# Feature-major gated attention, two heads to a product, and products of ones ahead of the first data

## The chip, the core and the metric

The kernel runs on one core of one Trainium2 chip. The metric is the time of one execution on the device in microseconds (us), from its first to its last instruction and the little that lies around them; the profile's span is that stretch without what lies around it. Everything is float32 at the interface.

## What is computed

A decoder trunk of two layers on 512 tokens with 1,024 features. Layer 0 is the one that the change touches most. Its mixer projects the normed tokens with one matrix, and the columns go to two mixers: gated linear attention (GLA: 4 heads, 64 key and 128 value features, chunks of 64 tokens) and differential attention (4 heads, two softmax maps each). Layer 1 is a dilated sliding-window attention. After each mixer comes a gated MLP with a causal convolution of width 3. The GLA, cut from the reference:

```
qc, kc, vc, lc = chunk(q * (dk ** -0.5)), chunk(k), chunk(v), chunk(log_a)   # chunks of 64 tokens
b = jnp.cumsum(lc, axis=3);  b_last = b[:, :, :, -1:, :]
q_d = qc * jnp.exp(b);  k_d = kc * jnp.exp(-b)
att = jnp.where(causal, einsum('bhnik,bhnjk->bhnij', q_d, k_d), 0.0)
kv = einsum('bhnjk,bhnjv->bhnkv', kc * jnp.exp(b_last - b), vc)
state = exp(b_last) * state + kv                                             # scan over chunks
o = att @ vc + q_d @ state
log_a = log_sigmoid(ar @ w_a2 + b_a) / 16                                    # ar: 16 low-rank features
oa = rmsnorm(o, gla_gain) * silu(ag)
```

The root mean square of a token scales its row of every projection; it is applied after the product.

## The kernel before, in words

**Precision and products.** Each large product is made from three float32r products: every operand is split into a rounded part and the rest (`hi`, `lo`), and hi x hi, lo x hi and hi x lo are added up in one PSUM bank. `split` (line 198) does it with one ScalarE copy and one vector subtraction; `load_next` (166) does the same for each slab of weights, 128 x 1024 in most cases, that a transfer on SP's queue brings. Three raw, three hi and three lo slabs are held, and `slab` (186) keeps two loads ahead. The small products of the attentions are plain float32; each of them is two instructions in the trace, a transpose is one.

**Order.** TensorE's instructions run in the order in which the program issues them; the other engines' order is laid out by the framework. The program interleaves the attentions with the projections by a queue of events: `at(delay, fn, tag)` (279) puts a function into a heap at a time `now + delay`, `pe(us)` (287) lets `now` go on by the planned cost of products, `run` (290) issues a projection step by step and, after each step, fires what is due, and `drain` (295) fires the rest of one kind. `now` is a count of planned TensorE work, and no clock.

**Token-major projections** (`tok_gemm`, 303): tokens are the stationary side, 512 weight columns move, four banks hold the four tiles of 128 tokens; in each of the four slabs the tiles are the outer loop, the slab's two chunks of features the inner one. A step is one tile of one slab, six products. **Feature-major projections** (`feat_gemm`, 325): weights are the stationary side, the 512 tokens move; 24 products for 8 chunks go to one bank. Its step is one bank.

**Start** (435 to 456). On SP's queue come the small parameters, the first 128 x 512 chunk of x, the first slab in two halves, the other seven chunks of x and two slabs between them. Each chunk of x is split with its gain into `hhi`, `hlo` before the projections want it; sums of squares are collected in `sqacc` (223), and a product with a column of ones (`Rstd`, 232) gives the reciprocal root by token. For the MLPs `rstd_rows` (248) gives the same as a row on all partitions: a float32 product of a 128 x 128 matrix of ones with `sqacc`, then six passes of 512 columns on the vector engine and ScalarE.

**Mixer of layer 0** (694 to 710). Projections in the order: differential values, queries, keys, GLA keys and queries (`aqk`), half the gates with the 16 low-rank features, GLA values, the other half of the gates; then the output projection in two halves of eight banks with 12 products each, for the differential and for the GLA heads. The softmax events (`diff_scores`, `diff_tr`, `diff_pv`, 486 to 535) run among them, and behind the last of them the GLA events start, once for each tile n of 128 tokens (two chunks):

- `decay1`, `decay2`, `decay3` (555 to 586) run earlier: they transpose the low-rank features, multiply them with `w_a2`, take the log-sigmoid and split it into `la`. `decay3` multiplies each head's log decay, laid out twice (`y2`), with two columns of constants; ScalarE's exponent of it is `dd`, the decay of a whole tile and of its first chunk.
- `gla_sums(n)` (590): eight products of 256 columns with constant triangles as the stationary side (`tri`) and `la` moving give the decay sums, tokens on partitions. Two exponents (`ee`, `eb`), then six vector products with `aqk`: keys and queries, each laid out twice for the two chunks (`ks`, `qs`), and keys for the state (`kd`). Five planned us later follows `gla_tr`, six later `gla_sums(n + 1)`.
- `gla_tr(n)` (621): eight transposes, one copy each by ScalarE and the vector engine; three planned us later
- `gla_att(n)` (628): four products of 128 x 128, one masked copy (`copy_predicated`) into zeros that GpSimd has written; three planned us later, or once values and gates are there,
- `gla_out(n)` (655): four products with the values, for n > 0 four more with the scaled state `Ss`, a copy to `o`; for n < 3 four products `kd` x values and the state's update (four vector instructions), then the scaled state (four); last `head_norm` (467) with its transposes 7.5 planned us later.

The tiles of these events come from one ring of nine buffers of 512 columns (`t2`, 404); in the GLA part eight of them are taken per n.

## Time and profile before

| | |
|---|---|
| median of 3 runs | 1244.42 us (1244.16 to 1244.56) |
| the profiled execution's own time | 1244.83 us |
| its span | 1242.7 us, 15158 instructions |
| TensorE busy | 1230.5 us (99%) |
| vector engine busy | 765.5 us (62%) |
| ScalarE busy | 542.7 us (44%) |
| DMA | 114.56 MB, 92 GB/s on the mean |

The shares are means over stages with different limits. Products are pipelined, so the busy time of one that stands in the trace is longer than the distance from its start to the next one's; distances between starts are what adds up on TensorE. Engine names in the rows: PE is TensorE, PEld its weight loads, DVE the vector engine, ACT ScalarE, POOL GpSimd, SP the queue that issues transfers. `bank` is a PSUM bank.

### The profile page before, as it was taken

What the parts mean: (1) busy time and instruction counts of PE and PEld (TensorE: products, weight loads), DVE (VectorE), ACT (ScalarE), POOL (GpSimd) and SP (SyncE); (2) the same over time, 40 slices, a digit from 0 to 9 for tenths busy, and PEclk for the clock granted to TensorE, in tenths of its full rate; (3) what the DMA queues carried; (4) which work ended last, traced back from release to release, by engine and by line L of the source; (5) the groups of instructions that cost most, each with busy time, mean ns of one, the idle gap of its engine ahead of it and who ended that gap; (6) DMA issues with size and microseconds to landing.
All of it is one profiled execution on the core that took longest, in us unless ns stands there. A gap on an engine that the chain in (4) does not pass through costs nothing.

```text
span 1242.7 us, 15158 instructions
## 1 busy us (share of the span) xinstructions
PE 1230.5 (99%) x5870; PEld 1021.5 (82%) x5870; DVE 765.5 (62%) x1405; ACT 542.7 (44%) x891; POOL 16.5 (1%) x35
## 2 busy tenths in 40 slices
PE   8999999999999999999999999999999999999998
PEld 6887788888888888888888888889888888888887
DVE  6457768777753776366845565543787536773673
ACT  5446554454432443234634554444544324442341
POOL 0000000000000000000000000300000000000000
PEclk9999999999999999999999999999999999999999
DMA  7222121223323332332422223421223323333322
GB/s 249 89 87 68 35 65 38 85 85 102 103 88 99 102 99 88 102 98 64 136 85 87 85 68 102 106 83 51 93 94 102 102 88 99 102 93 94 102 76 93
DMA packets 34487, 114.56 MB, mean 92 GB/s; under 512 B 4423, under 2 KB 5096, under 8 KB 34416
## 3 DMA queue, kind: packets, MB, share of 16 engines
q1 hardware_dynamic: 32256, 110.38, 28.0%
q10 hardware_dynamic: 1296, 2.10, 0.5%
q0 software_dynamic: 864, 1.12, 0.4%
q8 instruction: 46, 0.75, 0.3%
q14 instruction: 25, 0.20, 0.0%
HBM read 110.41 MB, written 2.12 MB: 91 GB/s over the span
## 4 chain that ended last, share of the span: by engine, by line
PE 96%; DVE 2%; DMA 1%; ACT 1%; issue 0%; POOL 0%; SPq 0%; DVEq 0%; ACTq 0%; POOLq 0%
PE bank L720 39%; PE bank L316 26%; PE bank L762 19%; PE bank L332 5%; PE bank L362 2%; PE bank L943 1%; PE bank L493 1%; PE bank L527 1%; PE bank L928 1%; PE bank L866 1%; PE bank L855 0%; PE bank L515 0%; DMA xT<-in_xT_dram 0%; DVE lo L180 0%; ACT p L499 0%; PE bank L584 0%
## 5 line engine op out<-in xcount | busy, mean ns | idle before, releaser
L177 ACT ACTIVATE hi<-raw 128x1024 fp32r<-128x1024 f32 (+2 forms) x209 | 217.1, 1040 | 324.1 <-PE bank L762 143.2
L180 DVE TENSOR_TENSOR lo<-raw,hi 128x1024 fp32r<-128x1024 f32 (+2 forms) x209 | 250.6, 1199 | 155.9 <-ACT hi L177 148.5
L720 PE MATMUL bank<-hhi,hi 128*128 128x512 f32 x704 | 274.7, 390 | 0.0
L720 PE MATMUL bank<-hlo,hi 128*128 128x512 f32 x704 | 273.9, 389 | 0.0
L720 PE MATMUL bank<-hhi,lo 128*128 128x512 f32 x704 | 273.9, 389 | 0.0
L316 PE MATMUL bank<-hi,hhi 128*128 128x512 f32 (+2 forms) x512 | 201.6, 394 | 5.7 <-ACT hi L177 5.5
L316 PE MATMUL bank<-lo,hhi 128*128 128x512 f32 (+2 forms) x512 | 194.7, 380 | 0.0
L316 PE MATMUL bank<-hi,hlo 128*128 128x512 f32 (+2 forms) x512 | 194.4, 380 | 0.0
L720 PEld LDWEIGHTS bank<-hhi,lo 128*128 128x128 f32 x704 | 132.1, 188 | 28.1 <-issue 0.5
L720 PEld LDWEIGHTS bank<-hhi,hi 128*128 128x128 f32 x704 | 132.1, 188 | 27.8 <-issue 0.5
L720 PEld LDWEIGHTS bank<-hlo,hi 128*128 128x128 f32 x704 | 132.1, 188 | 27.4
L762 PE MATMUL bank<-ghi,lo 128*128 128x512 f32 (+1 forms) x358 | 138.0, 385 | 0.0
L762 PE MATMUL bank<-glo,hi 128*128 128x512 f32 (+1 forms) x358 | 138.0, 385 | 0.0
L762 PE MATMUL bank<-ghi,hi 128*128 128x512 f32 (+1 forms) x358 | 138.0, 385 | 0.0
L316 PEld LDWEIGHTS bank<-hi,hhi 128*128 128x128 f32 x512 | 97.3, 190 | 23.1 <-ACT hi L177 5.5
L316 PEld LDWEIGHTS bank<-lo,hhi 128*128 128x128 f32 x512 | 97.0, 190 | 18.7 <-DVE lo L180 0.2
L316 PEld LDWEIGHTS bank<-hi,hlo 128*128 128x128 f32 x512 | 97.4, 190 | 16.2 <-DVE hlo L205 0.5
L767 DVE TENSOR_TENSOR xT<-xT,bank 128x512 f32<-128x512 f32 (+1 forms) x49 | 33.1, 676 | 106.4 <-PE bank L762 106.1
L762 PEld LDWEIGHTS bank<-ghi,lo 128*128 128x128 f32 x358 | 67.2, 188 | 13.6
L762 PEld LDWEIGHTS bank<-ghi,hi 128*128 128x128 f32 x358 | 67.2, 188 | 13.5
L762 PEld LDWEIGHTS bank<-glo,hi 128*128 128x128 f32 x358 | 67.2, 188 | 13.4
L201 ACT ACTIVATE ghi<-cv 128x512 fp32r<-128x512 f32 x44 | 27.8, 631 | 109.4 <-DVE cv L745 109.4
(192 smaller groups left out, 1288.4 us busy)
## 6 DMA issues: line engine op xcount, KB each, us to landing
raw<-in_weights_dram SPq DMA_DIRECT2D x189, 512.0 KB, 3.5
raw<-in_weights_dram SPq DMA_DIRECT2D x16, 384.0 KB, 3.1
xT<-in_xT_dram SPq DMA_DIRECT2D x8, 256.0 KB, 5.3
out_dram<-xT ACTq DMA_DIRECT2D x7, 256.0 KB, 2.0
raw<-in_weights_dram SPq DMA_DIRECT2D x2, 544.0 KB, 3.6
vt<-vs POOLq DMA_DIRECT2D x16, 64.0 KB, 4.1
raw<-in_weights_dram SPq DMA_DIRECT2D x2, 256.0 KB, 3.5
tr<-in_consts_dram SPq DMA_DIRECT2D x1, 256.0 KB, 4.4
```

The lines of the kernel that those rows point to most:

```text
L177: r = A.activation(hi[:, c0:c1], raw[:, c0:c1], AF.Copy)
L180: V.tensor_tensor(out=lo[:, c0:c1], in0=raw[:, c0:c1], in1=hi.bitcast(F32)[:, c0:c1], op=ALU.subtract)
L201: A.activation(hi, src, AF.Copy)
L316: T.matmul(ps[t][:, :n], lhs(a[:, kc], t), b[:, k, :n], start=(kc == 0 and j == 0), stop=(kc == DC - 1 and j == 2))
L332: T.matmul(ps, w[:, k, d * P:(d + 1) * P], r(k), start=(k == 0 and j == 0), stop=(k == nk - 1 and j == 2))
L362: T.transpose(pt[:, h * P:(h + 1) * P], src[:, h * P:(h + 1) * P], ident)
L493: T.matmul(sc[:, :nk], qT[rs, h, n * P:(n + 1) * P], kT[rs, h, :nk], start=True, stop=True)
L527: T.matmul(po[n][:, h * P:(h + 1) * P], wT[:, j * P:(j + 1) * P], bv[:, j, h * P:(h + 1) * P], start=(h == 0 and j == 0), stop=(h == 3 and ...
L720: T.matmul(ps, w[:, kc], r[:, kc], start=(kc == 0 and m == 0), stop=(kc == DC - 1 and m == 2))
L762: T.matmul(ps[:, ts], a[:, k], b[f0 + k][:, ts], start=(k == 0 and m == 0), stop=(k == n - 1 and m == 2))
L767: V.tensor_tensor(out=xT[:, c, ts], in0=xT[:, c, ts], in1=ps[:, ts], op=ALU.add)
L866: T.matmul(sc[:, hs], q[:, h, ts], k[:, h, ts], start=(h == 0), stop=(h == 3))
```

## The change

Its parts, in the order of the diff:

1. The constants' four triangles are laid out anew as four blocks of 128 columns that all move; the columns that `decay3` and the doubled keys and queries needed are gone.
2. The weight slabs of `aqk` are cut by 128 columns and all 1,024 features, for a feature-major projection.
3. A memset fills the last chunk of `hhi` with ones, and nine products of 512 columns with it go into a bank that nobody reads, ahead of all others.
4. `rstd_rows` splits `sqacc` into float32r parts and makes two float32r products with a float32r matrix of ones, in place of one float32 product.
5. The first projection goes chunk by chunk in its first slab (all four tiles of chunk 0, then of chunk 1; the product with the low part of the weights is second); its step there is two products' worth of tiles. `feat_gemm` with eight chunks has four steps to a bank.
6. The first chunk of x comes and is split in two halves, the first slab's load between them.
7. `rows_begin` is an event of layer 0 (nine planned us after the fourth slab of the first projection, the product five later), which makes the row of reciprocal roots; the feature-major `aqk` is scaled with it by the vector engine when a bank is read.
8. `decay3` and `gla_tr` are gone. In `gla_sums` `la` is the stationary side and 512 columns of constants move, twice for each pair of heads f. One exponent, then short vector products for each f: keys for the two chunks, keys for the state (n < 3), queries for each chunk and head of the pair, with the other head's half of the partitions left zero (`qd`), queries for the state (n > 0); the tile's decay is a column of the exponent. Two transposes stay for the state's keys (n < 3). Scores are four products, two of them with 64 stationary columns. Four masked copies take the place of one. State products are of two heads at once, 256 columns, and only the halves that belong together are read; the scaled state is gone. A tile takes six buffers of the ring.

```diff
@@ constants @@
-C_E0, C_E1, C_B, C_SU, C_W0, ... = (C_KEEP + i * P for i in range(11))
+C_TR, _, _, _, C_W0, ... = (C_KEEP + i * P for i in range(11))
...
+    c[:, C_TR:C_TR + 4 * P] = np.concatenate([e0[:, :64], e1, su, b[:, 64:], b[:, :64], cu[:, 64:]], axis=1)
@@ weight_slabs @@
-        tok("ev_w_in", c0, n)
+        if c0 == 0:
+            slabs.extend(("ev_w_in", 0, 0, DC, c * P, P) for c in range(4))
+        else:
+            tok("ev_w_in", c0, n)
@@ trunk_kernel @@
+    V.memset(hhi[:, DC - 1].bitcast(F32), 1.0)
+    warm = bank()
+    for _ in range(9):
+        T.matmul(warm, hhi[:, DC - 1, :P], hhi[:, DC - 1], start=True, stop=True)
+    onesr = per.tile([P, P], F32R, name="onesr")
+    V.memset(onesr.bitcast(F32), 1.0)
-    def rstd_rows():
+    def rstd_rows(hi, lo, parted=False):
         pb = bank()
-        T.matmul(pb, ones.to_broadcast([P, P]), sqacc[0], start=True, stop=True)
+        if not parted:
+            split(hi, lo, sqacc[0], None)
+        for i, v in enumerate((hi, lo)):
+            T.matmul(pb, onesr, v, start=(i == 0), stop=(i == 1))
@@ tok_gemm @@
+            by_chunk = chunkwise and s == 0
+            for step in range(kper * NT // 2):
+                for u in range(2):
+                    k, t = divmod(2 * step + u, NT) if by_chunk else ((2 * step + u) % kper, (2 * step + u) // kper)
...
+                    for j, (a, b) in enumerate(((hhi, whi), (hhi, wlo), (hlo, whi)) if by_chunk else
+                                               ((hhi, whi), (hlo, whi), (hhi, wlo))):
@@ the start @@
-                nc.sync.dma_start(xT[:, c], x[c])
...
+                for t in ((slice(0, 2 * P), slice(2 * P, S)) if c == 0 else (slice(0, S),)):
+                    nc.sync.dma_start(xT[:, c, t], x[c, :, t])
+                    if i == 0:
+                        split(hhi[:, c, t], hlo[:, c, t], xT[:, c, t], gmix[0][:, c:c + 1])
+                    if c == 0 and t.start == 0:
                         load_next()
...
+        def rows_begin():
+            hi, lo = (t2([P, 512], f"sq{x}").bitcast(F32R) for x in ("hi", "lo"))
+            split(hi, lo, sqacc[0], None)
+            at(5.0, lambda: rows.append(rstd_rows(hi, lo, True)), "params")
@@ decay2, decay3 @@
-            y2 = t2([P, 4, 2, 64], "y2")
-            for u in range(2):
-                V.scalar_tensor_tensor(out=y2[:, :, u], in0=heads(y), scalar=0.0, in1=heads(e), ...)
-            split(heads(la[:, t, 0]), heads(la[:, t, 1]), y2[:, :, 0], None)
-            at(4.0, lambda: decay3(t, y2), "gla")
...
+            V.scalar_tensor_tensor(out=y, in0=y, scalar=0.0, in1=e, op0=ALU.min, op1=ALU.subtract)
+            split(la[:, t, 0], la[:, t, 1], y, None)
@@ gla_sums, gla_att @@
+            ks = [t2([P, 512], f"ks{f}") for f in range(2)]
+            for f in range(2):
+                px = bank()
+                for m in range(2):
+                    T.matmul(px, la[:, n, m, f * P:(f + 1) * P], tri, start=(m == 0), stop=(m == 1))
+                ee = t2([P, 512], f"ee{f}")
+                A.activation(ee, px, AF.Exp)
+                q, k = aqk[:, f, ts], aqk[:, 2 + f, ts]
+                V.tensor_tensor(out=ks[f][:, :64], in0=ee[:, :64], in1=k[:, :64], op=ALU.mult)
+                V.tensor_tensor(out=ks[f][:, 64:192], in0=ee[:, 64:192], in1=k, op=ALU.mult)
+                if n < NT - 1:
+                    V.tensor_tensor(out=ks[f][:, 192:320], in0=ee[:, 192:320], in1=k, op=ALU.mult)
+                for c in range(2):
+                    e0 = 320 + 64 * (1 - c)
+                    for e in range(2):
+                        rs = slice(64 * e, 64 * e + 64)
+                        V.tensor_tensor(out=qd[rs, f, c, e], in0=ee[rs, e0:e0 + 64], in1=q[rs, c * 64:c * 64 + 64], ...)
+                if n > 0:
+                    V.tensor_tensor(out=ks[f][:, 320:448], in0=ee[:, 384:512], in1=q, op=ALU.mult)
+                V.tensor_copy(dd[:, n, f:f + 1], ee[:, 511:512])
...
+            at(5.0, lambda: gla_att(n, ks), "gla")
...
+            for f, c in ((0, 1), (0, 0), (1, 0), (1, 1)):
+                T.matmul(pav[:64 * (c + 1), f, c], ks[f][:, 64 * c:64 + 128 * c], qd[:, f, c].rearrange(...), ...)
@@ gla_out @@
+            if n > 0:
+                for f in range(2):
+                    T.matmul(po[:, f * 256:f * 256 + 256], ks[f][:, 320:448], St[:, f].rearrange("p e v -> p (e v)"), ...)
...
+                for f in range(2):
+                    T.matmul(pv[:, f * 256:f * 256 + 256], kd[:, f], av[:, n, f * 256:f * 256 + 256], ...)
```

## Rows read from the trace of the kernel before

**Rows 1.** The page: busy time, share of the span and instructions of TensorE (part 1), and the shares of the chain that ended last, by engine (part 4).
```profile
PE 1230.5 (99%) x5870; PEld 1021.5 (82%) x5870; DVE 765.5 (62%) x1405; ACT 542.7 (44%) x891; POOL 16.5 (1%) x35
...
PE 96%; DVE 2%; DMA 1%; ACT 1%; issue 0%; POOL 0%; SPq 0%; DVEq 0%; ACTq 0%; POOLq 0%
```

**Rows 2.** Busy time by stretch. Columns: stretch (us), its length, then busy us and number of instructions of TensorE (PE), its weight loads (PEld), the vector engine (DVE), ScalarE (ACT) and GpSimd (POOL); granted TensorE clock, share of the DMA engines' time, GB/s.
```profile
0.00:5.47 5.47, 0.00 (x0) 0.00 (x0) 1.65 (x9) 2.63 (x3) 0.89 (x5) 1.00 0.59 180
5.47:13.87 8.40, 8.13 (x17) 5.54 (x18) 6.63 (x9) 7.86 (x12) 0.00 (x0) 1.00 1.04 382
...
107.40:176.05 68.65, 66.77 (x408) 52.29 (x407) 51.05 (x152) 41.15 (x109) 0.00 (x0) 1.00 0.16 47
176.05:231.60 55.55, 54.61 (x378) 49.75 (x377) 46.54 (x109) 24.94 (x43) 2.10 (x4) 1.00 0.18 58
```

**Rows 3.** The list of waits of TensorE from 0 to 255 us. Columns: who waits at which line <- for whom: us in total, times, longest.
```profile
PE bank L515 <- DVE p L505: 1.4, 1, 1.4
PE bank L631 <- DVE xT L338: 0.8, 1, 0.8
PE bank L493 <- ACT dd L586: 0.3, 1, 0.3
...
PE bank L659 <- DVE rs_u L214: 0.2, 1, 0.2
```

**Rows 4.** Instructions in order of time at the start. Columns: start us, us, engine, line, operation, out<-in, count, idle time before it.
```profile
4.79 0.63 ACT L177 ACTIVATE hi<-raw 128x512 fp32r<-128x512 f32 x1 [0.27 <-DMA raw<-in_weights_dram]
...
12.61 0.63 PE L316 MATMUL bank<-lo,hhi 128*128 128x512 f32 x1
...
13.03 0.63 PE L316 MATMUL bank<-hi,hhi 128*128 128x512 f32 x1
...
14.34 0.39 PE L316 MATMUL bank<-hi,hlo 128*128 128x512 f32 x1
...
14.57 0.40 PE L316 MATMUL bank<-lo,hhi 128*128 128x512 f32 x1
```

**Rows 5.** The chain of waits in order of time, one piece of the first MLP: start us, us, what.
```profile
265.28 87.09 PE bank L720 x384
```

**Rows 6.** Instructions in order of time while the low-rank decay is computed (columns as in rows 4).
```profile
126.53 0.95 PE L584 MATMUL bank<-cst,y 128*128 128x2 f32 x8
127.41 0.92 PE L493 MATMUL bank<-kT,qT 64*128 64x384 f32 x4
...
139.53 0.18 ACT L586 ACTIVATE dd<-bank 128x8 f32<-128x8 f32 x1 [2.11 <-PE bank L584]
```

**Rows 7.** Instructions in order of time in the GLA part (columns as in rows 4): the transposes of tile 0, the sums of tile 1, the state product of tile 1.
```profile
182.77 0.60 PE L362 MATMUL bank<-cst,ks 128*128 128x128 f32 x4
...
183.64 0.60 PE L362 MATMUL bank<-cst,qn 128*128 128x128 f32 x4
...
184.00 1.20 PE L595 MATMUL bank<-la,tri 128*128 128x256 f32 x8
...
185.03 0.28 PE L316 MATMUL bank<-hi,hhi 128*128 128x256 f32 x1
...
205.32 1.06 PE L670 MATMUL bank<-av,kd 128*128 128x128 f32 x8
...
206.21 1.06 PE L631 MATMUL bank<-qsT,ksT 128*128 128x128 f32 x8
```

**Rows 8.** Two score products of the differential attention with a contraction of 64 rows, and what follows on TensorE (columns as in rows 4).
```profile
132.97 0.92 PE L493 MATMUL bank<-kT,qT 64*128 64x384 f32 x4
133.81 0.38 PE L527 MATMUL bank<-bv,wT 128*128 128x128 f32 x1
```

**Rows 9.** The vector engine's groups from 176.05 to 217.85 us, shapes apart. Columns: line, engine, operation, out<-in, shapes, count | busy us, mean ns of one | idle time before them.
```profile
L610 DVE SCALAR_TENSOR_TENSOR qs<-eb,cst,aqk 128x256 f32<-128x256 f32 x8 | 3.7, 480 | 0.0
L635 DVE COPY_PREDICATED att<-cst,bank 128x512 f32<-128x512 int32 x4 | 2.9, 733 | 1.1 <-PE bank L631 1.1
L625 DVE COPY qsT<-bank 128x512 f32<-128x512 f32 x4 | 2.8, 688 | 0.1
...
L680 DVE TENSOR_SCALAR Ss<-St,scl 128x128 f32<-128x128 f32 x12 | 2.6, 282 | 0.0
L616 DVE TENSOR_TENSOR kd<-eb,aqk 128x256 f32<-128x256 f32 x6 | 2.3, 420 | 0.0
L677 DVE SCALAR_TENSOR_TENSOR St<-St,dd,bank 128x128 f32<-128x128 f32 x8 | 2.2, 343 | 0.1
```

**Rows 10.** Busy time by stretch within the GLA part (columns as in rows 2).
```profile
176.05:182.77 6.72, 6.72 (x59) 6.72 (x57) 4.69 (x14) 2.44 (x5) 0.00 (x0) 1.00 0.22 78
...
203.53:210.75 7.22, 7.22 (x55) 6.66 (x53) 7.16 (x20) 1.83 (x5) 1.05 (x2) 1.00 0.22 75
...
222.50:231.50 9.00, 9.00 (x45) 7.51 (x44) 6.26 (x12) 2.74 (x5) 0.00 (x0) 1.00 0.29 96
```

**Rows 11.** ScalarE's SiLU of the gates and the table load behind it (columns as in rows 4).
```profile
193.54 1.92 ACT L686 ACTIVATE ag<-ag 128x2048 f32<-128x2048 f32 x1
...
195.47 1.28 ACT L687 ACT_TABLE_LOAD   x1
```

**Rows 12.** TensorE at the row of reciprocal roots of the first MLP (columns as in rows 4).
```profile
264.26 1.02 PE L251 MATMUL bank<-sqacc,cst 128*128 128x512 f32 x2
...
265.36 0.40 PE L720 MATMUL bank<-hhi,lo 128*128 128x512 f32 x1
```

More of the change, by code (lines that the diff above doesn't have):

```diff
@@ L612, in gla_sums, with gla_att @@
+            pe(0.91)
+            at(5.0, lambda: gla_att(n, ks), "gla")
+            if n < NT - 1:
+                at(GTICK, lambda: gla_sums(n + 1), "gla")
+        def gla_att(n, ks):
             kd = None
             if n < NT - 1:
[L614 to L619 removed]
@@ L692, in late, with ev_qk @@
             at(8.0, lambda: scaled(bv, r0)(t, ps), "params")
-        run(tok_gemm(512, nat, late, before))
+        run(tok_gemm(512, nat, late, before, chunkwise=True))
         run(tok_gemm(512, nat, qk_evict(qT, g_dqk, 8, r0, "diff")))
         run(tok_gemm(512, nat, qk_evict(kT, None, 8, r0, "diff", after_k)))
-        run(tok_gemm(512, nat, scaled(aqk, r0)))
+        for d in range(4):
+            def ev_qk(_, ps, d=d):
+                if d < 2:
+                    V.scalar_tensor_tensor(out=aqk[:, d], in0=ps, scalar=0.125, in1=rows[0], op0=ALU.mult, op1=ALU.mult)
+                else:
+                    V.tensor_tensor(out=aqk[:, d], in0=ps, in1=rows[0], op=ALU.mult)
+            run(feat_gemm(DC, P, lambda k: hhi[:, k], lambda k: hlo[:, k], ev_qk))
         run(tok_gemm(272, nat, agr_evict))
@@ L791, in ffn @@
             p0 = up(0), up(NF)
-            bc = rstd_rows()
+            bc = rstd_rows(*(fp.tile([P, S], F32R, name=f"sq{x}", bufs=1) for x in ("hi", "lo")))
             p1 = up(1), up(NF + 1)
```

150 lines of the change are left out of this document (58 added, 92 removed).

## The prediction

> **What bounds the kernel now.** I read the page first: TensorE is busy for 1230.5 of 1242.7 us, and the chain that ended last is TensorE for 96% of it [rows 1]. So only three things move the end: work that leaves TensorE, idle time in front of it, and its clock. The profiled execution took 1244.83 us, 2.1 around its span, and the median of the runs is 1244.42, 0.4 below; I take my sum off the median. About 0.2% (2.5 us) is the least that a measurement of this kernel tells from no change.
>
> Then the stretches that the diff touches [rows 2]. In the first, the 17 products up to 13.87 us take 8.40 us. In the last two the vector engine is busy for 51.05 of 68.65 and 46.54 of 55.55 us. The list of waits gives TensorE 1.4, 0.8, 0.3 and 0.2 us of idle time behind other engines up to 255 us, besides the first product's own [rows 3]. It is small, but it lies just in the stretches from which work is taken.
>
> **The start: products of ones, halved x, order by chunk.** Before 13.87 us two products of 512 columns start 0.42 us apart, after it 0.23 [rows 4]; in a long stretch 384 of them take 87.09 us, 0.227 each [rows 5]. That is 512 columns at 1.2 and at 2.4 GHz, though the granted-clock column of [rows 2] says 1.00 throughout. 17 products at 0.227 would be 3.9 us, so 4.5 us is the most that the clock and the gaps among them can give.
> The first product waits until 5.47 us, for the cast of the first half slab that begins at 4.79 [rows 4]. The memset and the nine products of ones (9 x 0.43 = 3.8 us) can run from about 1.5 to 5.3, before any data is there. The real ones then begin at about 5.4, as before; the halved x brings them perhaps 0.3 forward, and I don't count it. It costs SP's queue one issue more and puts the second half of that chunk behind both halves of the first slab; the second half's products are third in line, so they aren't late. The memsets of the two state tiles (1,536 columns, an estimated 1.6 us) fit into the first 5.47 us, of which the vector engine is busy for 1.65 [rows 2]. If the level rises as long after the first product as it did before (8.4 us), it does so at 9.9. By then 10 real products are through, and the other 86 take 19.5: 29.4 in place of 13.87 + 79 x 0.227 = 31.8. That is **-2.4**. Bounds: the ones count for nothing and only the order helps, -0.3; the level rises before the first real product, and then the transfers decide (their engines' share is 1.04 there [rows 2]) and some 3.5 are gained. I take the value from the one delay that rows show.
>
> **The decay sums by themselves go** (`decay3`, four groups of eight instructions). One group holds TensorE from 126.53 to 127.41, 0.88 us [rows 6]; the others have the same form: 4 x 0.86 = -3.4. ScalarE's exponent behind it (L586) kept that engine idle for 2.11 us before it could run [rows 6], with the next softmax's exponent queued behind it; this is the 0.3 that L493 waits for `dd` and, I think, half of the 1.4 that L515 waits for [rows 3]. -1.0 for those, bounds 0 (less cover in front of the same transposes gives it back) and -1.7. **Together -4.4.** The second copy of the gates (four vector products) goes too, and costs nothing either way.
>
> **Feature-major keys and queries.** 96 products of 512 columns become 96 of 512. Four evictions leave ScalarE and four come to the vector engine, at some 0.7 us, one every 5.4 us of products: each has its own bank, so nobody waits. New is the row of reciprocal roots: a split, two float32r products, and six passes of 512 columns, due some 40 us before the first eviction wants it. What shows is the two products, 0.46, and the break in the stream: **+0.6**. If that cover were gone the passes would be 4 us once.
>
> **Chunk by chunk (the GLA part), on TensorE.** Before, each tile has eight transposes: two groups of four from 182.77 to 183.64, so 0.87 a tile, 3.5 in all [rows 7]; two of them stay in three tiles, 0.65: -2.8. The sums: 184.00 to 185.03 for eight products of 256 [rows 7] against four of 512, 0.91: -0.4 over four tiles. Scores stay at four products of 128 columns, and the state and output products at the same columns, fewer and longer (205.32 to 206.21 for eight): -0.3. TensorE is 54.6 without its 0.94 of waits; so it would need 54.6 - 3.5 = 51.1 us for what takes 55.55 now.
> Two score products a tile have a stationary of 64 columns, which no row of before has. The nearest are those of 64 rows: 0.84 us for two products (132.97 to 133.81 [rows 8]), where their 4 x 384 columns are 0.64 at 2.4 GHz. So a change of shape costs 0 to 0.2 here; I take 0.1 a tile, +0.4, and 51.5 us. The Trainium skill (TensorEngine Tiling (Array Packing), "Key Properties") says that a change of tiling mode drains the engine. By that, two changes a tile at the 0.2 of [rows 8] would make it +1.6 and the sum 1.2 worse; the row agrees that there is such a price.
>
> **The same on the vector engine.** Here 54 instructions become 96, mostly shorter. By means in [rows 9], before: twelve scaled products at 0.48 and ten plain ones at 0.42, four copies at 0.69, four masked ones at 0.73, the state one copy at 0.69 and 8 x 0.34, the scaled state 12 x 0.28, three tiny copies: 23 us. After: from 0.42 at 256 and 0.28 at 128 columns 64 columns are an estimated 0.21. 68 small products and copies then make 15.4, sixteen masked copies an estimated 0.31 (0.73 less 384 columns) 5.0, the state 3.8: 24.2. Neighbours overlap by up to 0.09 (twelve of 0.282 are busy for 2.6 [rows 9]), so the busy time becomes 44 (all of them overlap) to 48 (those that go from one half of the partitions to the other don't), from 46.5. I take 46.
> The idle time of 9.0 us there can't all be used: 2.0 lies in the first stretch, before the first sums are through, 2.7 in the last, when GLA is done [rows 10], and some 2 while ScalarE does the SiLU with its two table loads (the SiLU 1.92, a load 1.28 [rows 11]): 6.5 to 7. 46 + 6.5 = 52.5 against 51.5: a new wait of 1.0. In the middle the engine is already full: 7.16 of 7.22 us [rows 10].
> A second new wait lies in the ring of nine buffers. A tile now takes six of them, in the order keys, keys, exponents, exponents, keys transposed, scores. By the event queue's own costs the sums of tile 2 are issued ahead of the output of tile 1, and the second exponent of tile 2 gets the buffer that this output still reads; so with tile 3 and the output of tile 2. The scores come 1.1 us behind that output and need the exponent (0.6) and half the products (1.1): about 1.0 late, twice: 2.0. **Waits of 3.0 in place of 0.94**, bounds 0 and 7.5 (48 + 9.0 - 51.5 + 2). Part sum: 51.5 + 3.0 - 55.55 = **-1.0**.
>
> **The two rows in the MLPs.** L251 holds TensorE from 264.26 until the second product behind it starts at 265.36 [rows 12]: 1.10 less one product of 0.23 is 0.87; two float32r products are 0.45. Twice: **-0.8**. The split before them is hidden by the 24 products of the second up-projection chunk, 5.4 us; without that cover it costs 1.3 a time.
>
> Sum: -2.4 - 4.4 + 0.6 - 1.0 - 0.8 = -8.0; 1244.4 - 8.0 = **1236.4**.
>
> **Rivals.**
> *The vector engine becomes the bound of the GLA part, and the kernel gets slower.* Place: the 96 short instructions between the first sums and the last output. If the fixed part of a short instruction is larger than from [rows 9], every 0.1 on it is 9.6 us on an engine that is already full there. It decides from 8.0 + 2.5 = 10.5 us on, 0.32 us an instruction in place of 0.21. With 0.37, 0.16 x 96 = 15.4: 1251.8. For it: 7.16 of 7.22 [rows 10]. Against: the 128-column row is 0.28 in full, and the tiny ones of four columns would have to be longer. 0.04.
> *Halves of the partitions don't overlap.* 32 query products and 12 state updates alternate between the halves. Without the overlap of 0.09 they keep the engine 44 x 0.09 = 4.0 us longer than if all overlap; 48 in place of 46 makes the wait 5.0 and the time 1238.4. The Trainium skill (VectorE: DVE Perf Modes, "Two Vector instructions with no wait between them") has this rule: an instruction whose operands start in another group of 32 partitions than those before starts only when they have finished. No run here shows it yet. 0.20.
> *The ones don't raise the clock earlier.* Then the start gives 0.3: 1238.5; with a long GLA wait as well (7.5) 1243.0, no change. 0.12, 0.05 of it at no change.
> *GLA has no waits.* The buffers come free in time: 1233.4. For it: before, only 0.94 in all. 0.16.
> *It doesn't do what it says:* the order of events hides the decay groups' gain in new waits of the softmax chain (stalls of 1.4 become 3 to 4): 1240. 0.08.
>
> **Numbers.** My forecast has 0.40, the rivals 0.04, 0.20, 0.12, 0.16 and 0.08. All but the first of them and the part of the clock case that ends at no change lie between 1232.5 and 1241.0; that leaves out under 2 in 10, with extremes that add up (-3.5 and -1.7 at once, or 7.5 and no clock). Faster by over 0.2% (below 1241.9) 0.90, within 0.06, slower 0.04.
>
> **What would show it.** Products of 512 columns 0.227 apart from some 10 us on and 1.2 GHz spacing only before; the first projection done at about 30.2 in place of 32.6. No L584 rows; TensorE's wait behind `dd` gone. From the first sums to the last product of half 0 some 54.5 us, vector engine busy for about 46 of them, and the waits of TensorE in front of the score products of tiles 2 and 3, with an exponent that waits for an output product as their cause. Two products in place of L251. I am wrong if the clock rises at 13.9 again, if short vector instructions take 0.3 us or more, or if TensorE waits for over 8 us in the GLA part.

## The result, and the profile after

The changed kernel takes 1238.26 us (median of four runs, 1237.69 to 1238.49), where the kernel before took 1244.38 beside it (1244.16 to 1244.56): ratio 0.9949, 95% interval 0.9935 to 0.9963. That is 6.1 us where 8.0 were forecast. The profiled execution took 1238.14 us, its span is 1236.3, 6.4 less than before. Page, parts 1 and 4, of the kernel after (answers to [rows 1]):

```profile
PE 1227.1 (99%) x5783; PEld 1014.7 (82%) x5783; DVE 771.9 (62%) x1458; ACT 540.9 (44%) x888; POOL 16.4 (1%) x35
...
PE 94%; DVE 3%; ACT 1%; DMA 1%; issue 0%; SPq 0%; POOL 0%; DVEq 0%; POOLq 0%; ACTq 0%
```

TensorE is busy for 3.4 us less, and its part of the chain went from 96 to 94%: some of the end is now set by other engines. Where the 6.4 us come from is told by five marks: the first real product, the eight tiny products that give the first reciprocal roots by token (84 of the first projection's 96 products stand before them; "the roots" below), the first score product of the softmax attention, the first decay sum, the first product of half 1. From the last of them on, both kernels need the same 32.64 us to the first MLP's row. The two long stretches that differ most, after the change (columns as in [rows 2]):

```profile
87.93:169.31 81.38, 80.98 (x467) 62.15 (x467) 61.65 (x197) 48.67 (x130) 0.52 (x1) 1.00 0.18 54
169.31:226.20 56.89, 53.65 (x313) 45.48 (x311) 47.48 (x152) 23.71 (x42) 1.57 (x3) 1.00 0.19 56
```

| part | before, us | after, us | change | forecast |
|---|---|---|---|---|
| start, to the roots | 29.09 | 26.93 | -2.16 | -2.4 |
| the roots, to the first softmax scores (the new row's two products lie here) | 60.54 | 61.00 | +0.46 | +0.6 |
| softmax attention and decays | 86.42 | 81.38 | -5.04 | -4.4 |
| GLA part | 55.57 | 56.89 | +1.32 | -1.0 |
| two rows in the MLPs | 2 x 0.87 | 2 x 0.45 | -0.84 | -0.8 |

They add up to -6.3; the span says -6.4. Four of the five terms came out within 0.7 us. The GLA part became longer instead of shorter, 2.3 us from its term; the other four are 0.6 better together, so the sum misses 1.7. TensorE's waits up to 255 us (answers to [rows 3]; the ones' wait for their memset lies before any data):

```profile
PE bank L684 <- DVE att L658: 1.5, 2, 1.2
PE bank L224 <- DVE hhi L221: 1.5, 1, 1.5
PE bank L684 <- DVE rr L218: 1.4, 1, 1.4
PE bank L333 <- DVE lo L182: 0.5, 1, 0.5
PE bank L544 <- DVE p L534: 0.3, 1, 0.3
PE bank L650 <- DVE qd L627: 0.2, 1, 0.2
```

The softmax attention's waits (1.4 and 0.3 in [rows 3]) are down to 0.3 (L544); 3.1 us of new ones stand in the GLA part (it had 1.0), nearly all in front of L684, the output products. The start, instructions in order of time (columns as in [rows 4], to which they answer):

```profile
1.46 4.21 PE L224 MATMUL bank<-hhi 128*128 128x512 f32 x9 [1.46 <-DVE hhi L221]
...
5.46 0.63 PE L333 MATMUL bank<-hi,hhi 128*128 128x512 f32 x1
...
7.43 0.39 PE L333 MATMUL bank<-lo,hhi 128*128 128x512 f32 x1
...
7.65 0.39 PE L333 MATMUL bank<-hi,hlo 128*128 128x512 f32 x1
...
13.67 0.50 PE L333 MATMUL bank<-lo,hhi 128*128 128x512 f32 x1 [0.53 <-DVE lo L182]
```

With the ones the product spacing is down to 0.22 us, the 2.4 GHz level, at 7.4 us, and not from 13.9 on as before. The last row shows what that meets: a product that waits for its data.

### The profile page after: what moved, and what is told of

It is laid out like the page before. It is cut to its first block, busy times and chain, and to the rows that moved or that the text cites. A ratio compares the mean times of both kernels' runs of the same rounds, so it can differ in the third digit from the quotient of the medians.

```text
span 1236.3 us, 15020 instructions
## 1 busy us (share of the span) xinstructions
PE 1227.1 (99%) x5783; PEld 1014.7 (82%) x5783; DVE 771.9 (62%) x1458; ACT 540.9 (44%) x888; POOL 16.4 (1%) x35
## 4 chain that ended last, share of the span: by engine, by line
PE 94%; DVE 3%; ACT 1%; DMA 1%; issue 0%; SPq 0%; POOL 0%; DVEq 0%; POOLq 0%; ACTq 0%
PE bank L752 39%; PE bank L333 23%; PE bank L794 19%; PE bank L350 7%; PE bank L382 1%; PE bank L975 1%; PE bank L522 1%; PE bank L960 1%; PE bank L898 1%; PE bank L556 1%; PE bank L887 0%; DMA xT<-in_xT_dram 0%; DVE lo L182 0%; PE bank L544 0%; DVE qd L627 0%
## 5 line engine op out<-in xcount | busy, mean ns | idle before, releaser
L179 ACT ACTIVATE hi<-raw 128x1024 fp32r<-128x1024 f32 (+2 forms) x209 | 217.1, 1040 | 315.9 <-PE bank L794 143.2
L333 PE MATMUL bank<-hi,hhi 128*128 128x512 f32 (+2 forms) x480 | 187.0, 390 | 0.0
L333 PE MATMUL bank<-lo,hhi 128*128 128x512 f32 (+2 forms) x480 | 181.5, 378 | 0.5 <-DVE lo L182 0.5
L333 PE MATMUL bank<-hi,hlo 128*128 128x512 f32 (+2 forms) x480 | 180.7, 376 | 0.1
L333 PEld LDWEIGHTS bank<-lo,hhi 128*128 128x128 f32 x480 | 90.4, 188 | 18.3 <-DVE lo L182 1.4
L333 PEld LDWEIGHTS bank<-hi,hhi 128*128 128x128 f32 x480 | 90.7, 189 | 16.0 <-issue 0.9
L333 PEld LDWEIGHTS bank<-hi,hlo 128*128 128x128 f32 x480 | 90.6, 189 | 15.1 <-DVE hlo L207 0.5
```

The costliest lines, as they stand in the source:

```text
L179: r = A.activation(hi[:, c0:c1], raw[:, c0:c1], AF.Copy)
L333: T.matmul(ps[t][:, :n], lhs(a[:, kc], t), b[:, k, :n], start=(kc == 0 and j == 0), stop=(kc == DC - 1 and j == 2))
```

## The experiments

Each run stands beside runs of the kernel before on the same chip (medians 1245.0 us for e1, e2, e4 and e7, 1244.73 for e3, e5, e6 and e8, 1244.9 for the rest). Stretches and marks are those of the table. The intervals of the ratios are 1 to 2 us wide to either side, so variants of the changed kernel can't be told apart by their times alone. The starts of kernels whose start is the same differ by up to 1.2 us (the roots come at 25.9 to 27.2), but a later part with the same code repeats: the GLA part is 56.89 in the changed kernel, 56.92 in e1 and 56.93 in e12, and 55.57 to 55.59 in the four profiles that have the old one. So a part is compared by its own length, of one profiled execution each.

### What the start is worth: e1, e12 and e8

e1 takes the ones out of the changed kernel:

```
-    V.memset(hhi[:, DC - 1].bitcast(F32), 1.0)
-    warm = bank()
-    for _ in range(9):
-        T.matmul(warm, hhi[:, DC - 1, :P], hhi[:, DC - 1], start=True, stop=True)
```

> The changed kernel without the memset and the nine products of ones. Theory (the ones bring TensorE's 2.4 GHz forward): the 427 ns spacing lasts until 13 to 14 us again, the eight tiny products of the first root mean square begin at about 28.8 us in place of 26.93, and the time is 1240.1 us against 1238.3. Rival (the new order and the halved x gave the gain, the clock nothing): they begin within 0.4 us of 26.93, and the time is 1238.3 to 1238.7.

Measured: 1239.15 us (1238.59 to 1239.61), ratio 0.9954 (0.9939 to 0.9969), which no measurement here tells from 0.9949. Two stretches of its start (columns as in [rows 2]); in the first, products start 0.42 to 0.43 us apart from the third on, in the second 0.22 to 0.24 (the clock column reads 1.00 for both, so the level is told by the spacing):

```profile
5.09:10.41 5.32, 5.32 (x12) 3.92 (x13) 3.33 (x6) 3.75 (x7) 0.00 (x0) 1.00 0.95 326
10.41:26.92 16.51, 16.51 (x74) 13.63 (x73) 15.04 (x23) 11.80 (x18) 0.00 (x0) 1.00 0.84 291
```

The roots come at 26.92, as with the ones (26.93), so the rival held. The theory failed already at the clock: the level rises 3.0 us later than with the ones (10.41 instead of 7.38), but not at 13 to 14. Without the ones TensorE waits for nothing behind its first product; with them five products between 7.4 and 14 us start 0.33 to 0.93 us behind their forerunner though the level is up (the 13.67 above is the 0.93). The nine profiled kernels that have both the ones and the order by chunk reach the roots at 25.9 to 27.2, 26.56 on average; so up to some 0.4 us may belong to the ones, which one execution without them can't show.

Against the kernel before, e1 gains 2.17 at the roots: 0.38 by an earlier first product (5.09), 0.69 in the first six products (3.03 us, where they took 3.72 with the wait for the second chunk of x among them), and 1.1 because the level rises after 12 products and not 17. That last part is no sure merit of the order: in e7 and e11 below, which have the old start unchanged, the level rises at 11.4 and 11.7, and the roots come at 28.23 and 28.26. The 13.87 and 29.09 of the kernel before are the latest of three executions. Against e7 and e11 the order with the halved x gains 1.3.

e12 keeps the ones and the halved x and takes the order by chunk back (`run(tok_gemm(512, nat, late, before))` without `chunkwise=True`).

> The changed kernel with the first projection's old order (tile by tile in the first slab), ones and halved x kept. Theory (the order gives the start's gain, since without the ones it stayed): the eight tiny products of the first root mean square begin at 28 us or later, in place of 26.1 to 27.1. Rival (the early clock is enough by itself): 27.2 or earlier.

Measured: 1240.94 us (1239.21 to 1241.38), ratio 0.9967 (0.9954 to 0.9979). The roots come at 29.64, as the theory said, and later than in the kernel before, e7 and e11, which have neither (28.2 to 29.1). The wait for the second chunk of x, in the kernel before and in e12, and the stretch behind it in e12 (columns as in [rows 2]):

```profile
PE bank L316 <- ACT hhi L204: 0.3, 1, 0.3
...
PE bank L333 <- ACT hhi L206: 2.4, 1, 2.4
```

```profile
9.68:13.09 3.41, 3.24 (x8) 2.56 (x9) 2.37 (x4) 3.41 (x6) 0.00 (x0) 0.50 1.04 410
```

The ones raise the level early; the old order then asks for the second chunk of x before it is there, TensorE stands for 2.4 us, and the granted clock falls to 0.50, 1.2 GHz, until 13.09. Part of that wait is the halved x: ScalarE's cast of the second chunk, first in the kernel before, then in e12, where it waits for the transfer:

```profile
6.61 0.72 ACT L204 ACTIVATE hhi<-xT,prm 128x512 fp32r<-128x512 f32 x1
...
8.29 0.72 ACT L206 ACTIVATE hhi<-xT,prm 128x512 fp32r<-128x512 f32 x1 [0.27 <-DMA xT<-in_xT_dram]
```

So with the ones and the halved x in both, the order by chunk is worth 2.7 us at the roots (29.64 to 26.93), and 2.2 by the medians, each off the kernel before on its chip (e12 -3.96, the changed kernel -6.12); the ones, with the order in both, are worth 0.3 (e1 -5.85), which is within the noise. Most of what the start gains is the order's, together with the halved x. The old order with the ones and a whole first chunk wasn't run, so what the ones do by themselves isn't shown.

e8 gives the kernel before the start and the float32r rows in the MLPs alone, and nothing else of the change.

> The kernel before with the start alone (ones, halved x, order by chunk) and the float32r rows of the MLPs; GLA, its projection and its decays as before. Theory (the parts add up: start -2.2, rows -0.8): 1241.4. Rival (what the start gains is taken back by a later wait, or the GLA part hides it): 1243 or more.

Measured: 1241.81 us (1241.36 to 1242.13), ratio 0.9978 (0.9968 to 0.9987), near the theory's 1241.4. The roots come at 27.15 (-1.94), the softmax part takes 86.41 and the GLA part 55.59 as before, the span is 2.7 shorter: -1.94 and twice -0.42 are -2.8. These two parts of the change add up, and neither touches the others. By the medians (-2.92, less 0.84 for the rows) the start is worth 2.1 us.

### What the decays are worth: e7 and e11

e7 is the kernel before without the decay sums (`dd` is set to 1.0):

```
+        V.memset(dd, 1.0)
...
-            at(4.0, lambda: decay3(t, y2), "gla")
```

> The kernel before without the decay sums by themselves (decay3) and the second copy of the gates; the decay of a whole tile is left out, ones stand in its place. Theory (ScalarE's exponent behind these products also held up the softmax chain): TensorE loses 3.4 us of products and most of the 1.7 us that it waits for dd and for L515's input: 1239.3 to 1240.0. Rival (the products alone): L515's wait of 1.4 us stays or grows, 1241.0 or more.

One thing in that expectation didn't hold of the kernel: the second copy of the gates stayed in e7. It goes in e11 (`for u in range(1)` in `decay2`, besides the edit above).

> The kernel before without decay3 and this time without the second copy of the gates (ones stand for the decay of a whole tile). Theory (the second copy stood ahead of the softmax on the vector engine): the stretch from the first softmax scores to the first sums falls by 5.0 us as in the changed kernel, 81.4 in place of 86.4, and the time is 1239.5 on the other runs' base of 1244.5. Rival (the changed kernel's other order, without four ScalarE evictions of keys and queries, did it): 84 us as with decay3 alone out, 1242.

Measured: e7 1242.43 us (1241.03 to 1243.33), ratio 0.9979 (0.997 to 0.9989), e11 1241.31 (1239.82 to 1242.56), ratio 0.9973 (0.9963 to 0.9982). The softmax part is 84.12 in e7 and 82.82 in e11, from 86.42: -2.3 and -3.6. e7 came out as its rival said (the products alone, 1241.0 or more), e11 between its theory (81.4) and its rival (84). e7 in order of time, where [rows 6] and [rows 8] had two score products in 0.84 to 0.92; first TensorE and its weight loads, then the vector engine:

```profile
135.24 1.96 PE L493 MATMUL bank<-kT,qT 64*128 64x384 f32 x4
...
136.29 0.29 PEld L493 LDWEIGHTS bank<-kT,qT 64*128 64x128 f32 x2 [0.76 <-DVE nm L269]
...
140.35 0.55 PE L515 MATMUL bank<-cst,p 128*128 128x128 f32 x3 [1.62 <-DVE p L505]
```

```profile
134.85 0.42 DVE L576 SCALAR_TENSOR_TENSOR y<-ye 128x256 f32<-128x256 f32 x1 [0.86 <-ACT ye L573]
...
135.27 0.42 DVE L576 SCALAR_TENSOR_TENSOR y<-ye 128x256 f32<-128x256 f32 x1
...
135.68 0.55 DVE L269 CUSTOM_DVE_ANT_0 p<-bank,wide 128x384 f32<-128x384 f32 x1
```

The vector engine stands 0.86 us for ScalarE's gates, then makes both copies of them, and only then takes the softmax's scores out of their bank (L269). TensorE's next scores take 1.96 us, 1.0 more than a free pair, since the second of them waits for L269, and the wait behind L505 is 1.6, not shorter than before (1.4). So the products alone give 2.3; the second copies, which the forecast held to cost nothing, give another 1.3. In e11 TensorE's waits in this part are still

```profile
PE bank L515 <- DVE p L505: 1.2, 1, 1.2
PE bank L527 <- ACT wT L518: 0.3, 1, 0.3
```

and after the whole change 0.3. Of the 1.4 us by which the changed kernel is shorter yet, these waits are 1.2. Which of the other edits takes them away (ScalarE has four evictions fewer and is busy for 48.67 us of the part where e11 has 52.00; the events also come in another order) wasn't separated.

### Why the GLA part is longer: e2, e3, e9, and e4, e5, e6

First TensorE's own work. e2 gives all score products a stationary of 128 columns (the added columns are masked out anyway):

```
-                T.matmul(pav[:64 * (c + 1), f, c], ks[f][:, 64 * c:64 + 128 * c],
+                T.matmul(pav[:, f, c], ks[f][:, 64 * c:64 * c + 128],
```

> The changed kernel with 128 stationary columns in all four score products (the rows that come out in addition are not read). Theory (a change of the stationary's shape costs TensorE time): the score groups fall from 1.14 to 1.23 us to about 0.85; in tiles 0 and 1 that is gained, in tiles 2 and 3 it goes into the waits for the vector engine, so the time is 1237.4 to 1237.9. Rival (the group is long for another reason, its waits): the groups stay at 1.1 or more and the time at 1238.3.

Measured: 1237.42 us (1237.04 to 1238.38), ratio 0.9941 (0.9926 to 0.9956). The four score products of tile 0 and what follows them, first in the changed kernel, then in e2, in order of time:

```profile
176.20 1.39 PE L650 MATMUL bank<-qd,ks 128*128 128x128 f32 x8
...
177.43 0.60 PE L382 MATMUL bank<-cst,qn 128*128 128x128 f32 x4
```

```profile
175.38 1.06 PE L650 MATMUL bank<-qd,ks 128*128 128x128 f32 x8
...
176.27 0.60 PE L382 MATMUL bank<-cst,qn 128*128 128x128 f32 x4
```

From the first score to the next work it is 1.23 us with stationaries of 128, 64, 64 and 128 columns, and 0.89 with 128 throughout. The four tiles go from 1.23, 1.14, 1.22 and 1.89 to 0.89, 0.81, 0.89 and 1.50: 0.33 to 0.39 a tile, 1.4 in all, with the same streamed columns; so much the theory said. Yet e2's GLA part is 57.03 long, not shorter. The reason is in the granted clock (columns as in [rows 2]):

```profile
191.20:194.50 3.30, 3.30 (x11) 2.76 (x11) 3.12 (x17) 0.60 (x1) 0.53 (x1) 0.50 0.00 0
```

After a wait of 1.4 us at tile 1's output, where the changed kernel has one too, the level fell to 1.2 GHz for 3.3 us in this execution: the output and state groups L687 and L696 hold TensorE for 1.71 and 1.34 us, where the changed kernel has 0.87 each, and the output group before them (the second half of L684) for 0.90 instead of 0.55. That is 1.7; without it e2's part would be an estimated 55.4, which no run shows by itself.

e3 lets `kd` use the first exponent's buffer, so that a tile takes five buffers of the ring and not six (`kd = ee0[:, :2 * P]...` in place of `t2(...)`).

> The changed kernel with the transposed state keys written over the first exponent, so that a tile takes five buffers of the ring and none that a later output product still reads. Theory (the ring holds up the second exponent of tiles 2 and 3): the second exponent of tile 3 starts within 1 us of the first one (4.0 us behind it before), the wait of the scores of tile 3 goes, and 0.5 to 2 us are gained: 1236.3 to 1237.8. Rival (the vector engine is the bound and takes the exponent late anyway): within 0.3 of 1238.3.

Measured: 1237.04 us (1236.44 to 1237.18), ratio 0.9941 (0.9926 to 0.9956), GLA part 56.09, 0.8 shorter. The time is within the theory's range, but not for its reason. The two exponents of tile 3 are 4.05 us apart in e3 (below), and 4.03 in the changed kernel:

```profile
196.23 0.59 ACT L619 ACTIVATE ee<-bank 128x512 f32<-128x512 f32 x1
...
199.32 1.06 ACT L179 ACTIVATE hi<-raw 128x1024 fp32r<-128x1024 f32 x1 [0.39 <-PE bank L350]
...
200.28 0.58 ACT L619 ACTIVATE ee<-bank 128x512 f32<-128x512 f32 x1
```

ScalarE has the second exponent behind a cast (L179) of a weight slab, and that cast waits 0.39 us for a product of TensorE's (L350). The scores of tile 3 take 1.89 us in both. With fewer buffers the vector work came in another order, the wait of 1.4 at tile 1's output was gone, and one of 1.1 appeared at the transposes of tile 2. The ring theory fell.

Where the 1.4 comes from, the changed kernel shows itself, in order of time at the output of tile 1 (the last row is tile 3's):

```profile
186.38 1.92 ACT L712 ACTIVATE ag<-ag 128x2048 f32<-128x2048 f32 x1
...
188.32 1.28 ACT L713 ACT_TABLE_LOAD   x1
...
190.16 0.69 DVE L358 TENSOR_TENSOR xT<-xT,bank 128x512 f32<-128x512 f32 x1 [1.13 <-PE bank L350]
...
190.83 0.28 DVE L658 COPY_PREDICATED att<-cst,bank 64x128 f32<-64x128 int32 x1
...
191.53 0.68 PE L684 MATMUL bank<-av,att 128*128 128x128 f32 x4 [1.42 <-DVE rr L218]
...
192.51 0.71 PE L684 MATMUL bank<-av,att 128*128 128x128 f32 x4 [0.30 <-DVE att L658]
...
209.59 1.30 PE L684 MATMUL bank<-av,att 128*128 128x128 f32 x8 [1.24 <-DVE att L658]
```

ScalarE is held by the SiLU and its two table loads until 189.6. The norm's root (rs_y) comes after them. The vector engine stands idle until 190.16 in front of a residual sum, for TensorE's product, and the norm's remainder (L218) follows only then. The masked copies of tile 1 (L658) that the output products need stand among these, and now they are four small ones a tile where there was one large one. e3 shows that their place in this order makes the wait, and not the SiLU by itself: its second table load ends at 189.2, as late as here, but all four copies stand ahead of the residual sum, and the products run without a wait. e3 in order of time, the last copy and the output products of tile 1:

```profile
188.83 0.28 DVE L660 COPY_PREDICATED att<-cst,bank 128x128 f32<-128x128 int32 x1
...
189.59 1.05 PE L686 MATMUL bank<-av,att 128*128 128x128 f32 x8
```

At tile 3's output (209.59) it is the same engine, this time full: a wait of 1.24 for L658.

e9 tests whether the vector engine's load makes these waits: the query products of the second heads are left out (`for e in range(1)`), 16 instructions of 96.

> The changed kernel without the query products of the second head of each pair (16 of 32 short vector products; these scores come out as zeros). Theory (the vector engine's load bounds the tiles 2 and 3): 3.5 us leave it, the excess of the score group of tile 3 (1.89 in place of 1.2 us) and the wait of 1.24 in front of its output go, and the GLA stretch falls from 56.9 to 54.5 to 55.5 us: 1236 to 1237. Rival (ScalarE's SiLU and the order behind it set the pace): the stretch stays above 56.4 and the time at 1238.

Measured: 1235.15 us (1235.11 to 1237.45), ratio 0.9927 (0.9914 to 0.9941). Its GLA part (columns as in [rows 2]):

```profile
168.33:222.76 54.43, 52.72 (x313) 45.59 (x312) 42.88 (x136) 23.62 (x42) 1.57 (x3) 1.00 0.20 59
```

4.6 us less of vector work make the part 2.46 us shorter. That is what the theory said. The wait of 1.24 at tile 3's output is gone, and tile 3's scores take 1.22, not 1.89 (they waited for their query products). The 1.4 at tile 1's output stays, behind L218 as before: load has no part in it.

Three more edits try to relieve the vector engine. e4 has GpSimd make the query products (`G.tensor_tensor`); e5 has ScalarE square for the GLA norm; e6 pins half 0's residual sums to their place in the program (`tc.keep_in_program_order`), which was meant to put the masked copies ahead of them.

> The changed kernel with the 32 query products (qd) on GpSimd in place of the vector engine. Theory (the vector engine bounds the GLA part from tile 1's output on): its busy time between the first sums and the last product of half 0 falls from 47.5 by 6 to 7 us, TensorE's waits there from 3.1 to under 1, and the time is 1235.5 to 1236.5. Rival (TensorE's own order and shapes bound it): within 0.4 of 1238.3. Third case: GpSimd needs 0.5 us or more for each, the scores wait for it, and the time is 1240 or more.

Measured: 1238.63 us (1237.97 to 1238.84), ratio 0.9949 (0.9932 to 0.9965), GLA part 57.09. The busy time of the vector engine falls to 43.0, but GpSimd needs twice as long for each product (columns as in [rows 9]), where the changed kernel's vector engine has 7.0 us and a mean of 218 ns for the same 32:

```profile
L627 POOL TENSOR_TENSOR qd<-ee,aqk 64x64 f32<-64x64 f32 x32 | 13.3, 414 | 188.7 <-DVE ss L372 168.0 <-ACT ee L617 19.0
```

The vector engine has less to do, and still TensorE waits 2.1 us for masked copies at tile 1's output (1.7 and 0.4) and 0.3 for GpSimd at the scores of tile 3; the granted clock is at 0.50 for some 3.4 us from 194.1, as in e2.

> The changed kernel with the squares of the GLA heads' norm (512 columns, once a tile) on ScalarE in place of the vector engine. Theory (the vector engine bounds the GLA part): some 2.4 us leave it, TensorE's waits fall by 1 to 2 us, 1236.3 to 1237.3. Rival (its order, not its load: it stands still for the residual sum while masked copies are ready): within 0.4 of 1238.3.

Measured: 1238.0 us (1237.65 to 1239.04), ratio 0.9951 (0.9936 to 0.9966), GLA part 57.00. The vector engine is down to 44.8 busy, and TensorE has one new wait of 2.5 us, for ScalarE's rs_y behind the SiLU: the squares joined the queue that is late at tile 1. On load this says nothing.

> The changed kernel with the residual additions of the first half of the output projection held behind all earlier vector work in program order; nothing else differs. Theory (order: the vector engine waits 1.1 us for such a sum while the masked copies of tile 1 are ready, and TensorE waits 1.4 for them): that wait goes, 1236.8 to 1237.3. Rival (load): what is done earlier there is done later elsewhere, within 0.4 of 1238.3.

Measured: 1238.07 us (1237.98 to 1238.85), ratio 0.995 (0.9933 to 0.9967), GLA part 57.70, with the granted clock at 0.50 from 192.4 to 195.8. The residual sum is still ahead of tile 1's masked copies (189.70 against 190.38), as in the changed kernel: the pin moved nothing there, so e6 says nothing on order. None of the three shortened the GLA part, and their times are those of their rivals; as the load that was taken off came back elsewhere in e4 and e5, they don't weigh against e9.

### A version from what was found: e10

e2 and e3, the masked copies for both pairs of heads at once (8 in place of 16), the two key products in one (6 fewer; the last tile has only one of them), and the squares on ScalarE from tile 1 on:

```
+                V.tensor_tensor(out=heads(ks[f][:, 64:64 + m * P], m), in0=heads(ee[:, 64:64 + m * P], m),
+                                in1=k[:, None, :].to_broadcast([P, m, P]), op=ALU.mult)
...
+            for c in range(2):
+                rs = slice(0, 64 * (c + 1))
+                V.copy_predicated(out=att.rearrange("p (f e) n -> p f e n", f=2)[rs, :, :, c * 64:c * 64 + 64], ...)
```

> The changed kernel with 128 stationary columns in all score products, the state keys over the first exponent (five buffers of the ring a tile), masked copies for two pairs at once (8 in place of 16), the two key products in one (8 fewer), and the squares of the norm on ScalarE for tiles 1 to 3. Theory (the losses add up: 1.35 for the shape, 0.8 for the ring, 1 to 2 for the load): GLA stretch 53 to 54 us, 1234.5 to 1236.0. Rival (one wait takes the place of another): 55.5 or more, 1237 or more.

Measured: 1235.24 us (1234.68 to 1235.92), ratio 0.9924 (0.9911 to 0.9938), within the theory's range, and 3.0 us better than the changed kernel's median. Its GLA part (columns as in [rows 2]):

```profile
169.03:223.16 54.13, 51.97 (x313) 45.56 (x311) 44.62 (x135) 25.52 (x45) 1.57 (x3) 1.00 0.19 59
```

1.4 us below the kernel before in this part, with TensorE at 51.97 busy and 2.1 of waits left (1.2 at tile transposes, 0.9 behind a norm). What each of its edits gives wasn't separated.

## Why the prediction was right, and where only its sum was

**The start** (-2.4, measured -2.16): the right number for a wrong reason. The forecast took the time from the earlier rise of the clock, and gave the order by chunk 0.3. The level rose earlier still than it said (7.4, not 9.9). But e1 without the ones has the roots at the same time, and e12 with the ones in the old order has them at 29.64. Most of the gain is the order's, together with the halved x: the old one asks for the second chunk of x before it is there. What the early clock saves goes into waits for data. That the number came out is luck, also because the delay of 8.4 us on which it rests is one of several: with the old start the level rose 8.4, 5.7 and 6.1 us behind the first product (the kernel before, e7, e11). The rival that the ones raise no clock (0.12) is false as put, for the clock does rise earlier. What failed is the bound of -0.3 for the order alone. (The two state tiles have 1,024 columns to clear, 0.48 us for each 512, and not 1,536; nothing hangs on it.)

**The decays** (-4.4, measured -5.04): right in sum, wrong in two parts that offset each other. The eight-instruction groups weren't worth 3.4 and 1.0 of waits: without them alone it is 2.3 (e7), as TensorE then meets the softmax's scores in a bank that isn't emptied. And the second copy, "nothing either way", is worth 1.3 (e11): it stood on the vector engine in front of the instruction that empties that bank. The last 1.4 belongs to other edits, and which is open; so that the sum came out near is luck. The wait behind `dd` is gone, as said; the half of L515's 1.4 that was put down to it wasn't its doing, for e7 has 1.6 there.

**The row of roots** (+0.6, measured +0.46) and **the rows in the MLPs** (-0.8, measured -0.84): two products of 0.22 to 0.23 each, as worked out, and the splits hidden. In order of time after the change, second MLP (answers to [rows 12]):

```profile
883.85 0.39 PE L264 MATMUL bank<-sqhi,onesr 128*128 128x512 f32 x1
...
884.08 0.39 PE L264 MATMUL bank<-sqlo,onesr 128*128 128x512 f32 x1
...
884.30 0.39 PE L752 MATMUL bank<-hhi,hi 128*128 128x512 f32 x1
```

0.45 from the first to the next work, where [rows 12] gave 0.87.

**The GLA part** (-1.0, measured +1.3): the step that failed. It had TensorE at 51.5 and waits of 3.0. The listed waits are 3.2, near that size; TensorE is 53.65. Of those 2.1 us, 1.0 is the change of shape: the forecast took 0.1 a tile from [rows 8], e2 shows 0.33 to 0.39. The Trainium skill (TensorEngine Tiling (Array Packing), "Key Properties") has a drain at each change of tiling mode. The forecast gave +1.6 for that reading and decided against it; the runs give 1.4, near it. Whether it is the drain or something else of the narrower stationary that costs the time, e2 doesn't tell. Of the rest, 1.0 are waits that TensorE's busy time hides: 0.4 in the scores of tile 3 (1.89 where the others take 1.2, less the 0.2 that the list has), and 0.6 in the output products L684, which at tiles 1 and 3 take 0.3 and 0.25 longer than the 0.89 of tiles 0 and 2, besides the listed waits. e9 takes the 0.4 and the 0.25 away with the vector engine's work. So the waits are 4.2 in all, where 3.0 was forecast.

The waits came at other places than forecast and for other reasons. Not the ring (e3's exponents are as far apart as before), but the vector engine: at tile 1 its order, with the masked copies behind a residual sum that waits for TensorE (e3), and at tile 3 its load (e9). It is busy for 47.5, where 46 was taken and 48 set as the upper bound, and the chain of waits of the changed kernel runs through it from 190 us (start, us, what):

```profile
192.58 0.20 DVE ks L620
192.78 0.20 DVE ks L622
...
193.14 0.22 DVE qd L627
193.37 0.22 DVE qd L627
```

Key products of 128 partitions follow each other every 0.20 us, though one takes 0.28: they overlap. The query products that alternate between the halves follow every 0.23 and take 0.22: no overlap. e9, whose query products are all in one half, settles it; rows of the vector engine, first of the changed kernel, then of e9:

```profile
171.25 0.68 DVE L627 TENSOR_TENSOR qd<-ee,aqk 64x64 f32<-64x64 f32 x3
...
170.26 0.34 DVE L627 TENSOR_TENSOR qd<-ee,aqk 64x64 f32<-64x64 f32 x2
```

Three that alternate take 0.68, two in the same half 0.34 with 0.21 for each alone: the second starts 0.13 behind the first. So the mechanism of the rival "halves don't overlap" (0.20) is there, with the 47.5 near its 48, and its time of 1238.4 is nearest to what was measured. The Trainium skill (VectorE: DVE Perf Modes, "Two Vector instructions with no wait between them") says just that of instructions that start in another group of partitions, and the trace agrees. But its price was set at 5.0 of waits, and they are 4.2 with the hidden ones; its time agrees because the shape's 1.0 was missing on the other side.

The other rivals: GLA without waits (1233.4) is false, though e10 comes to 1235.24 by taking 1.1 of them and the change of shape away; the vector engine as a bound that makes the kernel slower is false, with 0.22 us for a short instruction where 0.32 would have decided; new waits in the softmax chain are false, there are fewer.

## What to carry to other kernels

Weigh a vector instruction not by its own time but by what stands behind it in its engine's order: the second copy of the gates, off TensorE's path by any count, held 1.3 us, and masked copies behind a residual sum another 1.4. When work moves from a full engine to one that is busy for 84% of a stretch already, count the moved work as a wait at both ends, and keep stationaries of one product group in one shape. An earlier clock is worth little (at most some 0.4 us here) where the next products' data isn't there: look first at whether the data or the clock comes later. And one profiled execution of a start is not enough: three of the same old start differ by 0.9 us.

## What the runs showed of the hardware that was not expected

The granted clock can fall after short waits, and not in each execution: to 0.50 for 3.3 us in e2 after TensorE stood for 1.4 us, in e4 (1.7) and e6 (1.4) at the same place, and in e12 after 2.4 us; the changed kernel's profiled execution has the same 1.42 and 0.30 and stays at 1.00, and so does e5 with a wait of 2.5. At 0.50 the output and state groups L687 and L696 of one tile cost 1.3 us more than at 1.00, so a wait's price here is larger than its length, and varies.

The level's first rise varies too: with the same old start it came at 13.9, 11.4 and 11.7 us.

Vector instructions of 64 partitions and 64 columns follow each other every 0.13 us in one half of the partitions (e9) and every 0.23 where they alternate between the halves.

A float32 group of four score products costs 0.33 to 0.39 us more when two of them have stationaries of 64 columns than when all have 128 (e2).
